# Reordering the start and the row products of a hybrid decoder trunk on one Trainium2 core

## The chip, the cores and the metric

One core of one Trainium2 chip. The metric is device time of one execution in microseconds; lower is better. The kernel before takes 2455.02 us, the median of three runs (2450.69 to 2460.17). Profiles are of one execution of their own.

## What is computed

Two decoder layers on 256 tokens of width 2048, float32, batch 1. Layer 0 mixes tokens with a causal Conformer convolution, layer 1 with gated linear attention; each is followed by a SwiGLU FFN of width 5632. Every sub-layer has a norm before and after it and a modulation (shift, scale, gate) that comes from a vector c:

```python
c_act = silu(c)
for i in range(2):
    mod = c_act @ w_ada[i] + b_ada[i]            # 6 * 2048 values
    sh1, sc1, gt1, sh2, sc2, gt2 = split(mod, 6)
    h = rms_norm(x, pre_mix_g[i]) * (1.0 + sc1) + sh1
    y = conformer_conv(h, ...) if i == 0 else gla_mixer(h, ...)
    x = x + gt1 * rms_norm(y, post_mix_g[i])
    h = rms_norm(x, pre_ffn_g[i]) * (1.0 + sc2) + sh2
    x = x + gt2 * rms_norm(swiglu_ffn(h, ...), post_ffn_g[i])

def conformer_conv(h, ...):
    a, g = split(h @ w_pw1 + b_pw1, 2)           # 2048 -> 2 * 2048
    u = a * sigmoid(g)
    u = depthwise_causal_conv(u, w_dw, width 31) + b_dw
    return silu(layer_norm(u, ln_g, ln_b)) @ w_pw2 + b_pw2
```

Only layer 0's mixer and the modulation vector of layer 0 are touched by the change.

## The kernel before

**Layout.** Activations lie transposed: 128 channels on the partitions, 16 channel blocks (KD), 256 tokens along the free axis. x, y and h are single tiles of this form; h has a high and a low half (`h_hi`, `h_lo`).

**Weights.** All weights come in tiles of 128 x 2048 float32 (1 MB) through one ring of six buffers (`rawp`, tag `raw`). A tile of a product is split into two halves, and each half into a rounded part and a remainder: ScalarE casts `hi` (L318), VectorE subtracts for `lo` (L319). A product is then three matmuls (hi·hi, hi·lo, lo·hi) in a faster float format. `next_half` hands the halves out in order and calls `pump`, which issues tiles a few halves ahead.

**One queue, one order.** All loads are issued from SyncE's queue (SP) in the order that `tile_order` writes out by hand: product tiles (`w`), tiles of w_ada for VectorE (`ada`), tiles of w_ada for TensorE (`rows`), and a few others. `spread` mixes one list evenly into another. Beyond this order a planner with its own cost model arranges the instructions of each engine; `issue_after` and `high_priority` bind it.

**Two ways to a modulation column.** A column is 128 values of mod. On VectorE, an `ada` tile holds 128 columns as rows of 2048, and one SCALAR_TENSOR_TENSOR (L300) multiplies by silu(c), spread over the partitions (`cb`), and sums along the row. On TensorE (`ada_rows`), a unit of two tiles, one pair of columns, is multiplied by silu(c) in 32 copies (`cc`): 16 matmuls of 256 columns into four groups of 32 partitions (L246), a copy to SBUF on ScalarE (L253), two small matmuls with `dup` that add the 32 copies back and turn the result into a column (L255), and an addition of the bias on VectorE (L261). In the head of layer 0 each unit gives block k's shift and scale together, and `modulate` follows (L451, L454, L455).

**Stages of layer 0's mixer.**

1. *Start.* Loads of c, taps, `turn`, x, parameters and bias; the taps are turned into the frequency domain by 12 matmuls on 31 partitions (L571) and stored in y and `h2`; x is squared and summed for the RMS norm (L582 to L592).
2. *Head.* For k = 0..15: row unit k, modulate block k of h, then its part of the three head chunks (4, 0, 5) of pw1. A chunk is 512 output channels; chunks 4 to 7 are the gates.
3. *Tail.* Chunks 1, 6, 2, 7, 3 of pw1, each over all k (L695 to L697). When a pair is done, `transform` makes u = a·sigmoid(g), a forward transform (L616), products with the taps' transform on VectorE (L625 to L633), and an inverse transform (L643 to L645). 18 VectorE columns are spread in between.
4. *LayerNorm* over channels (L707 to L735); row units for gt1 and part of sh2 lie at this place in the order.
5. *pw2* with the remaining row units and VectorE columns spread in; its first eight output blocks run side by side over k, the rest one after another; `gather` collects sums for the norms.
6. *Junction j0*, then FFN 0 and layer 1, which the change leaves as they are.

A row unit from the 17th on is not computed where its tile is issued: it is put on the list `waiting`, and `run_waiting` emits it when the products have come as far.

Of the kernel before, what the change touches and what calls it, by code (L numbers as in the profile page):

```python
# [14 lines left out]
P = 128  # L15
# [73 lines left out]
def tile_order():  # L89
# [6 lines left out]
    def rows(*units):  # L96
        return [("rows", u, half) for u in units for half in range(2)]
# [36 lines left out]
def trunk(ctx: ExitStack, tc: tile.TileContext, a: dict, out: bass.AP):  # L134
# [12 lines left out]
    crow = rawp.tile([P, D], F32, tag="raw", name="crow")  # L147
    nc.sync.dma_start(out=crow[:1, :], in_=a["c"])
# [12 lines left out]
    nc.sync.dma_start(out=x, in_=a["x"])  # L161
# [3 lines left out]
    braw = rawp.tile([P, TILE * P], F32, tag="raw", name="braw")  # L165
    nc.sync.dma_start(out=braw, in_=a["bpw1"])
    masks = const.tile([P, 8, P], I8, tag="masks", name="masks")
    cb = const.tile([P, D], F32, tag="cb", name="cb")
    for j in range(4):
        s = slice(j * 512, (j + 1) * 512)  # L170
        pc = ps.tile([P, 512], F32, tag="mm", name=f"cb{j}")
        nc.tensor.matmul(pc, ones[:1, :], crow[:1, s], start=True, stop=True)
        nc.scalar.activation(out=cb[:, s], in_=pc, func=AF.Silu)
# [25 lines left out]
    y = const.tile([P, KD, T], F32, tag="y", name="y")  # L199
# [38 lines left out]
    def ada_rows(raw, u, half):  # L238
        if half == 0:
            rows[u] = ps2.tile([P, 512], F32, tag="rb" if u < KD and u % 2 else "ss", name=f"ada{u}")  # L240
        bank = rows[u]
        wv = raw.rearrange("p (k n) -> p k n", n=T)
        for i in range(HALF):
            k = half * HALF + i
            j = 32 * (k % 4)
            nc.tensor.matmul(  # L246
                bank[j : j + 32, :T], cc[:, k, :], wv[:, i, :], start=k < 4, stop=k >= KD - 4
            )
        if half == 0:
            return  # L250
        rows.pop(u)
        flat = tmp.tile([P, T], F32, tag="sq", name=f"flat{u}", bufs=3)
        nc.scalar.copy(flat, bank[:, :T])  # L253
        for s in range(2):
            nc.tensor.matmul(  # L255
                bank[:, T + s : T + s + 1], flat[:, s * P : (s + 1) * P], dup, start=True, stop=True
            )
        n0, n1 = ROW_UNITS[u]
        sel = slice(n0, n1 + 1, n1 - n0)
        b_at = COLS["b_ada"][0]  # L260
        nc.vector.tensor_tensor(  # L261
            out=mod[:, sel], in0=bank[:, T : T + 2], in1=par[:, b_at + n0 : b_at + n1 + 1 : n1 - n0], op=ALU.add
        )
        if u < KD:
            nc.vector.scalar_tensor_tensor(
                out=der[:, 0, u : u + 1], in0=modcol(0, n1), scalar=1.0, in1=col("pre_mix_g", u),
                op0=ALU.add, op1=ALU.mult,
            )
            modulate(u, rbx, 0, 0, SH1)
            return  # L270
        have(0, n0 // KD, 2)
# [5 lines left out]
    def pump_one():  # L277
        kind, name, i = order[state["next"]]
        state["next"] += 1
        if kind == "waves":  # L280
            nc.sync.dma_start(out=fwd, in_=a["fwd"])
            nc.sync.dma_start(out=inv, in_=a["inv"])
            return
        raw = rawp.tile([P, TILE * P], F32, tag="raw", name=f"raw{state['next']}")
        if kind == "masks":
# [3 lines left out]
            return  # L289
        if kind == "rows":  # L290
            nc.sync.dma_start(out=raw, in_=a["w_ada_r"][name, i])
            if name < KD:
                ada_rows(raw, name, i)
            else:
                waiting.append((state["emitted"], lambda: ada_rows(raw, name, i)))
            return
        if kind == "ada":
            nc.sync.dma_start(out=raw, in_=a["w_ada"][name, i])
            with tc.issue_after(last_lo[0]) if last_lo else ExitStack():
                nc.vector.scalar_tensor_tensor(  # L300
                    out=raw, in0=raw, scalar=1.0, in1=cb, op0=ALU.mult, op1=ALU.mult, accum_out=modcol(name, i)
                )
            if i % KD == KD - 1:
                first = i - KD + 1
                if (name, i // KD) == (0, SH2):
                    first += sum(n // KD == SH2 for u in ROW_UNITS for n in u)
# [247 lines left out]
    bias_w = cv.tile([P, P], F32R, tag="bias_w", name="bias_w")  # L554
    nc.scalar.activation(out=bias_w, in_=ones, func=AF.Copy, scale=1.0 / 32)
    bias = cv.tile([P, TILE * P], F32R, tag="bias", name="bias")
    fwd = cv.tile([P, 2, F_COLS], F32, tag="fwd", name="fwd")
    inv = cv.tile([P, 3, T], F32, tag="inv", name="inv")
    mean_w = cv.tile([P, 32], F32, tag="mean_w", name="mean_w")
# [6 lines left out]
    for c in range(4):  # L566
        chans = taps[:, c * WIDE : (c + 1) * WIDE]
        for part in range(3):
            n = min(F_MAIN, F_COLS - part * F_MAIN)
# [479 lines left out]
```

## Time and profile before

| | us |
|---|---|
| median of three runs | 2455.02 |
| the profiled execution | 2462.36 |
| its span, first to last instruction | 2460.6 |
| PE busy | 2384.7 (97%) |
| VectorE busy | 1713.8 (70%) |
| ScalarE busy | 1115.1 (45%) |
| mean DMA rate | 246 GB/s |

The span is what the views of the trace count from; the profiled execution's own time is 1.8 us longer. PE's busy time counts pipelined matmuls whose ends are modelled, so a full PE may still have room. In rows of instructions the columns are line, engine, operation, written and read tiles, shapes, count, then busy time, mean nanoseconds of one, and the idle time before it with what ended it. In a timeline they are start, duration, engine, line, operation and tiles, with the idle time and its releaser in brackets. One float32 matmul appears as two records.

### The profile page before, as it was taken

The numbers are of one execution on the slowest core, as the hardware profiler recorded it, in microseconds if no ns is written. First come the engines' busy times: TensorE is split into PE (matmuls) and PEld (weight loads), VectorE is DVE, ScalarE is ACT, GpSimd is POOL, SyncE is SP. The second block draws the span as 40 slices with busy tenths as digits, with TensorE's granted clock in tenths as the row PEclk, the third lists the DMA queues.
The fourth block names the chain that finished last, engine by engine and source line by source line (L and its number), as shares of the span: only waits on it lengthen the run. The fifth ranks groups of instructions, "written<-read, shape, count | busy, mean of one in ns | idle before, by whom it ended". The sixth has DMA issues, their size and how long they took to land.

```text
span 2460.6 us, 35900 instructions
## 1 busy us (share of the span) xinstructions
PE 2384.7 (97%) x14480; PEld 2048.4 (83%) x14480; DVE 1713.8 (70%) x2436; ACT 1115.1 (45%) x1655; POOL 22.0 (1%) x26
## 2 busy tenths in 40 slices
PE   7989989899999999999999999999999999999997
PEld 2667758798888888888888989988988888888886
DVE  2448735887777677778986987898656655665665
ACT  3333325654444444444446545454444444444442
POOL 0000000000000000000000000000000000000001
PEclk9999999999999999999999999998999999999998
DMA  7986776847778778887844566773556656665651
GB/s 250 402 341 250 282 278 242 331 144 289 291 290 295 287 291 294 295 299 291 293 172 145 206 255 237 282 290 135 201 207 223 221 206 220 219 218 202 221 189 67
DMA packets 84504, 606.12 MB, mean 246 GB/s; under 512 B 9507, under 2 KB 9794, under 8 KB 11218
## 3 DMA queue, kind: packets, MB, share of 16 engines
q1 hardware_dynamic: 84338, 603.83, 67.3%
q8 instruction: 113, 1.85, 0.3%
q14 instruction: 53, 0.43, 0.0%
HBM read 601.70 MB, written 2.10 MB: 245 GB/s over the span
## 4 chain that ended last, share of the span: by engine, by line
PE 93%; DVE 3%; DMA 2%; ACT 1%; issue 1%; POOL 0%; POOLq 0%; SPq 0%; DVEq 0%; ACTq 0%
PE in L382 24%; PE out L382 13%; PE in L385 12%; PE out L385 7%; PE pw L695 3%; PE pw L696 2%; PE wo L382 2%; PE pw L697 2%; PE ada L246 2%; PE in_pair L355 1%; PE in_pair L356 1%; PE in_pair L357 1%; PE r L379 1%; PE r L380 1%; PE r L385 1%; PE wo L385 1%
## 5 line engine op out<-in xcount | busy, mean ns | idle before, releaser
L319 DVE TENSOR_TENSOR lo<-raw,hi 128x1024 fp32r<-128x1024 f32 x754 | 921.0, 1223 | 564.4 <-ACT hi L318 562.4
L318 ACT CAST hi<-raw 128x1024 fp32r<-128x1024 f32 x754 | 791.1, 1050 | 1073.3 <-issue 297.0
L382 PE MATMUL in<-h,hi 128*128 128x512 f32 x2560 | 900.0, 397 | 0.0
L385 PE MATMUL in<-h,lo 128*128 128x256 f32 x2560 | 716.3, 280 | 0.0
L382 PEld LDWEIGHTS in<-h,hi 128*128 128x128 f32 x2560 | 480.8, 188 | 117.4
L385 PEld LDWEIGHTS in<-h,lo 128*128 128x128 f32 x2560 | 482.8, 189 | 0.0
L382 PE MATMUL out<-m,hi 128*128 128x512 f32 x1364 | 477.3, 394 | 0.0
L385 PE MATMUL out<-m,lo 128*128 128x256 f32 x1408 | 392.0, 281 | 0.0
L300 DVE SCALAR_TENSOR_TENSOR raw<-raw,cb 128x2048 f32<-128x2048 f32 x136 | 310.6, 2284 | 4.8 <-DMA raw<-in_w_ada_dram 4.8
L382 PEld LDWEIGHTS out<-m,hi 128*128 128x128 f32 x1364 | 254.9, 188 | 58.4
L385 PEld LDWEIGHTS out<-m,lo 128*128 128x128 f32 x1408 | 264.1, 188 | 2.0
L695 PE MATMUL pw<-hi,h 128*128 128x512 f32 x256 | 101.9, 411 | 9.7 <-ACT h L454 9.7
L696 PE MATMUL pw<-lo,h 128*128 128x512 f32 x256 | 103.7, 406 | 0.0
L697 PE MATMUL pw<-hi,h 128*128 128x512 f32 x256 | 90.4, 396 | 0.0
L382 PE MATMUL wo<-oo,hi 128*128 128x512 f32 x240 | 83.7, 394 | 0.0
L355 PE MATMUL in_pair<-h,hi 128*128 128x256 f32 x256 | 71.4, 293 | 2.9 <-ACT h L454 2.9
L385 PE MATMUL r<-h,lo 128*128 128x256 f32 x256 | 73.2, 286 | 0.0
L379 PE MATMUL r<-h,hi 128*128 128x256 f32 x256 | 73.1, 286 | 0.0
L380 PE MATMUL r<-h,hi 128*128 128x256 f32 x256 | 72.9, 285 | 0.0
L356 PE MATMUL in_pair<-h,hi 128*128 128x256 f32 x256 | 72.6, 290 | 0.0
L695 PEld LDWEIGHTS pw<-hi,h 128*128 128x128 f32 x256 | 49.3, 193 | 27.2 <-ACT h L454 13.9
L385 PE MATMUL wo<-oo,lo 128*128 128x256 f32 x256 | 71.2, 281 | 0.0
(349 smaller groups left out, 2997.9 us busy)
## 6 DMA issues: line engine op xcount, KB each, us to landing
raw<-in_in_dram SPq DMA_DIRECT2D x176, 1024.0 KB, 5.0
raw<-in_w_ada_dram SPq DMA_DIRECT2D x136, 1024.0 KB, 5.3
raw<-in_out_dram SPq DMA_DIRECT2D x88, 1024.0 KB, 5.0
raw<-in_w_ada_r_dram SPq DMA_DIRECT2D x56, 1024.0 KB, 7.2
raw<-in_pw_dram SPq DMA_DIRECT2D x48, 1024.0 KB, 6.7
raw<-in_aqk_dram SPq DMA_DIRECT2D x17, 1024.0 KB, 4.9
raw<-in_v_dram SPq DMA_DIRECT2D x16, 1024.0 KB, 6.1
raw<-in_r_dram SPq DMA_DIRECT2D x16, 1024.0 KB, 5.8
```

The lines of the kernel that those rows point to most:

```text
L300: nc.vector.scalar_tensor_tensor(out=raw, in0=raw, scalar=1.0, in1=cb, op0=ALU.mult, op1=ALU.mult, accum_out=modcol(name, i))
L318: nc.scalar.copy(hi, part)
L319: done = nc.vector.tensor_tensor(out=lo, in0=part, in1=hi.bitcast(F32), op=ALU.subtract)
L355: nc.tensor.matmul(acc, w_hi, x_hi, start=opens, stop=False, skip_group_check=True)
L356: nc.tensor.matmul(acc, w_hi, x_lo, start=False, stop=False, skip_group_check=True)
L379: nc.tensor.matmul(acc[:, :T], w_hi[:, s], x_hi, start=n == 0, stop=False)
L380: nc.tensor.matmul(acc[:, :T], w_hi[:, s], x_lo, start=False, stop=False)
L382: nc.tensor.matmul(acc, w_hi[:, s], pair.rearrange("p a b -> p (a b)"), start=n == 0, stop=end, skip_group_check=True)
L385: nc.tensor.matmul(acc[:, :T], w_lo[:, s], x_hi, start=False, stop=end, skip_group_check=ob not in narrow)
L695: nc.tensor.matmul(accs[c][t], h_hi[:, k, n], w_hi[:, s], start=False, stop=False)
L696: nc.tensor.matmul(accs[c][t], h_hi[:, k, n], w_lo[:, s], start=False, stop=False)
L697: nc.tensor.matmul(accs[c][t], h_lo[:, k, n], w_hi[:, s], start=False, stop=k == KD - 1)
```

## The change

- **Loads first.** c goes into a part of y instead of a ring buffer; x follows at once, in four transfers. taps, `turn` and the bias of pw1 are issued between the k-tiles of the head, and the sums of squares of x use y as scratch, so that none of them takes a ring buffer at the start. taps and `turn` get a 32nd row of zeros. The bias comes as four rows into a tile that GpSimd has filled with zeros, and is added by a matmul in the middle of each accumulation (k = 12) instead of at its beginning.
- **Taps in the head.** The 12 taps matmuls become four steps (`taps_chunk`) after k = 4, 6, 8 and 10.
- **Scale on VectorE, shift on TensorE.** A row unit is now one tile with one column: 16 matmuls of 128 columns, one `dup` matmul. The 16 sh1 columns and the 16 gt1 columns go this way (32 units). The 16 sc1 columns, sc2 and sh2 go over VectorE: 16 in the head, 22 in pw1's tail, 10 in pw2.
- **Row products behind the inverse transform.** Six gt1 units are spread into the tail, four stand at its end and are held until the last inverse transform's last matmul, six lie in pw2. The last transform's inverse uses another PSUM bank.
- u, the gates' sigmoids and the taps share one tile (`share`).

```diff
-ROW_UNITS = [(k, KD + k) for k in range(KD)]
-ROW_UNITS += [(GT1 * KD + k, GT1 * KD + k + 1) for k in range(0, KD, 2)]
-ROW_UNITS += [(SH2 * KD + k, SH2 * KD + k + 1) for k in range(0, 8, 2)]
+ROW_COLS = [SH1 * KD + k for k in range(KD)] + [GT1 * KD + k for k in range(KD)]
...
     order = []
+    extra = {0: ["taps"], 2: ["waves"], 4: ["turn"], 5: ["bias"], 6: ["turn"], 8: ["turn"], 10: ["turn"]}
     for k in range(KD):
-        order += rows(k)
+        order += [("ada", 0, SC1 * KD + k)] + rows(k)
         order += [pw1[i] for i in range(lead) if 4 * i // len(HEAD_CHUNKS) == k]
-        if k == 2:
-            order += [("waves", 0, 0)]
-    late = ada(0, SC2) + ada(0, SH2)[8:]
-    units = range(KD, len(ROW_UNITS))
-    order += spread(pw1[lead:], late[:18])
-    order += rows(*units[:6])
-    order += spread(pw2[:12], rows(*units[6:]) + late[18:], 4) + pw2[12:]
+        order += [(kind, k, 0) for kind in extra.get(k, ())]
+    late = ada(0, SC2) + ada(0, SH2)
+    units = rows(*range(KD, len(ROW_COLS)))
+    order += spread(pw1[lead:], spread(late[:22], units[:6]), 1)
+    order += units[6:10] + spread(pw2[:14], units[10:] + late[22:], 2) + pw2[14:]
...
+    y = const.tile([P, KD, T], F32, tag="y", name="y")
+    crow = y[:1, KD // 2 :, :].rearrange("p a b -> p (a b)")
+    nc.sync.dma_start(out=crow, in_=a["c"])
...
-    taps = rawp.tile([P, TILE * P], F32, tag="raw", name="taps")[:WIDTH, :]
-    nc.sync.dma_start(out=taps, in_=a["taps"])
-    turn = early.tile([P, F_COLS], F32, tag="turn", name="turn")[:WIDTH, :]
-    nc.sync.dma_start(out=turn, in_=a["turn"])
...
-    nc.sync.dma_start(out=x, in_=a["x"])
+    for j in range(4):
+        nc.sync.dma_start(out=x[:, 4 * j : 4 * j + 4, :], in_=a["x"][:, 4 * j : 4 * j + 4, :])
...
-    braw = rawp.tile([P, TILE * P], F32, tag="raw", name="braw")
-    nc.sync.dma_start(out=braw, in_=a["bpw1"])
...
+    def ada_rows(raw, u):
+        bank = ps2.tile([P, 512], F32, tag="rb" if u < KD and u % 2 else "ss", name=f"ada{u}")
+        wv = raw.rearrange("p (k n) -> p k n", n=P)
+        for k in range(KD):
             j = 32 * (k % 4)
+            nc.tensor.matmul(bank[j : j + 32, :P], cc[:, k, :], wv[:, k, :], start=k < 4, stop=k >= KD - 4)
+        flat = tmp.tile([P, T], F32, tag="sq", name=f"flat{u}", bufs=3)[:, :P]
+        nc.scalar.copy(flat, bank[:, :P])
+        nc.tensor.matmul(bank[:, P : P + 1], flat, dup, start=True, stop=True)
+        n = ROW_COLS[u]
+        nc.vector.tensor_tensor(out=modcol(0, n), in0=bank[:, P : P + 1], in1=col("b_ada", n), op=ALU.add)
...
+        if kind == "taps":
+            nc.sync.dma_start(out=taps, in_=a["taps"])
+            nc.sync.dma_start(out=turn, in_=a["turn"])
+            return
+        if kind == "turn":
+            taps_chunk(turned.pop(0))
+            return
...
+        if kind == "bias":
+            nc.gpsimd.memset(raw, 0.0)
+            nc.sync.dma_start(out=raw[::32, :], in_=a["bpw1"])
+            nc.scalar.copy(bias, raw)
+            nc.vector.tensor_tensor(
+                out=bias[64:, :], in0=raw[64:, :], in1=bias[64:, :].bitcast(F32), op=ALU.subtract
+            )
+            return
...
+            if (name, i // KD) == (0, SC1):
+                k = i % KD
+                nc.vector.scalar_tensor_tensor(
+                    out=der[:, 0, k : k + 1], in0=modcol(0, i), scalar=b1[:, k : k + 1], in1=col("pre_mix_g", k),
+                    op0=ALU.add, op1=ALU.mult,
+                )
+                return
...
-            back = ps2.tile([P, 512], F32, tag="ss", name=f"back{half}")
+            if c == TAIL_CHUNKS[-1]:
+                back = ps.tile([P, 512], F32, tag="mm", name=f"back{half}")
+            else:
+                back = ps2.tile([P, 512], F32, tag="ss", name=f"back{half}")
...
-            u = cv.tile([P, 2, T], F32, tag="u", name=f"u{half}", bufs=2)
+            u = share[:, 2 * j * T : 2 * (j + 1) * T].rearrange("p (t n) -> p t n", t=2)
...
-    run_waiting(state["used"])
     while order[state["next"]][0] == "rows":
         pump_one()
-        if len(waiting) > 2:
-            waiting.pop(0)[1]()
-    run_waiting(state["used"])
+    with tc.issue_after(ends["inverse"]):
+        run_waiting(state["used"])
```

`taps_chunk` holds the three taps matmuls of one chunk of 512 channels and their copies on ScalarE, on the two PSUM banks that the row units use.

More of the change, by code (lines that the diff above doesn't have):

```diff
@@ L96, in rows @@
     def rows(*units):
-        return [("rows", u, half) for u in units for half in range(2)]
+        return [("rows", u, 0) for u in units]
     pw1, pw2 = w("pw1"), w("pw2")
@@ L171, in trunk @@
         pc = ps.tile([P, 512], F32, tag="mm", name=f"cb{j}")
-        nc.tensor.matmul(pc, ones[:1, :], crow[:1, s], start=True, stop=True)
+        nc.tensor.matmul(pc, ones[:1, :], crow[:, s], start=True, stop=True)
         nc.scalar.activation(out=cb[:, s], in_=pc, func=AF.Silu)
@@ L264, in ada_rows, with taps_chunk @@
         if u < KD:
[L265 to L268, printed above, removed]
             modulate(u, rbx, 0, 0, SH1)
-            return
-        have(0, n0 // KD, 2)
+        else:
+            have(0, n // KD, 1)
+    def taps_chunk(c):
+        chans = taps[:, c * WIDE : (c + 1) * WIDE]
+        for part in range(3):
+            n = min(F_MAIN, F_COLS - part * F_MAIN)
+            pt = ps2.tile([P, WIDE], F32, tag="rb" if part % 2 else "ss", name=f"taps{c}{part}")[:n, :]
+            nc.tensor.matmul(pt, turn[:, part * F_MAIN : part * F_MAIN + n], chans, start=True, stop=True)
+            if part == 2:
+                nc.scalar.copy(h2[:, c * WIDE : (c + 1) * WIDE], pt)
+            else:
+                nc.scalar.copy(
+                    y[:, 4 * c : 4 * c + 4, part * P : (part + 1) * P], pt.rearrange("p (b n) -> p b n", n=P)
+                )
@@ L552, in junction @@
         gate[:] = [end.ins]
-    bias_w = cv.tile([P, P], F32R, tag="bias_w", name="bias_w")
-    nc.scalar.activation(out=bias_w, in_=ones, func=AF.Copy, scale=1.0 / 32)
+    both_w = cv.tile([P, 2, P], F32, tag="both_w", name="both_w")
+    nc.vector.memset(both_w, 0.0)
+    for q in range(4):
+        nc.vector.memset(both_w[32 * q : 32 * q + 1, q % 2, :], 1.0)
+    bias_w = cv.tile([P, 2, P], F32R, tag="bias_w", name="bias_w")
+    nc.scalar.copy(bias_w, both_w)
     bias = cv.tile([P, TILE * P], F32R, tag="bias", name="bias")
@@ L558, in trunk @@
     inv = cv.tile([P, 3, T], F32, tag="inv", name="inv")
+    turn = cv.tile([P, F_COLS], F32, tag="turn", name="turn")[:32, :]
+    share = cv.tile([P, D], F32, tag="share", name="share")
+    taps = share[:32, :]
+    turned = list(range(4))
     mean_w = cv.tile([P, 32], F32, tag="mean_w", name="mean_w")
@@ L564, in trunk @@
         nc.vector.memset(v2[4 * F_REST : 4 * F_REST + 32, :], -1.0 / 32)
[L566 to L569, printed above, removed]
-            pt = ps.tile([P, WIDE], F32, tag="mm", name=f"taps{c}{part}")[:n, :]
-            nc.tensor.matmul(pt, turn[:, part * F_MAIN : part * F_MAIN + n], chans, start=True, stop=True)
-            if part == 2:
-                nc.scalar.copy(h2[:, c * WIDE : (c + 1) * WIDE], pt)
-            else:
-                nc.scalar.copy(
-                    y[:, 4 * c : 4 * c + 4, part * P : (part + 1) * P], pt.rearrange("p (b n) -> p b n", n=P)
-                )
-    sqs = [rawp.tile([P, TILE * P], F32, tag="raw", name=f"sqs{j}") for j in range(2)]
-    quarter = [sqs[j // 2][:, (j % 2) * 4 * T : (j % 2 + 1) * 4 * T] for j in range(4)]
+    quarter = [y[:, 4 * j : 4 * j + 4, :] for j in range(4)]
     for j in range(4):
-        nc.scalar.square(quarter[j], x[:, 4 * j : 4 * j + 4, :].rearrange("p a b -> p (a b)"))
+        nc.scalar.square(quarter[j], x[:, 4 * j : 4 * j + 4, :])
         if j % 2:
@@ L644, in inverse @@
                     nc.tensor.matmul(yi, vb[:, i, :], inv[:, 1, :], start=False, stop=False)
-                    nc.tensor.matmul(yi, v2[:rows, sel], inv[:rows, 2, :], start=False, stop=True)
+                    return nc.tensor.matmul(yi, v2[:rows, sel], inv[:rows, 2, :], start=False, stop=True)
                 if b == 0:
@@ L685, in trunk @@
                 accs[c] = [ps.tile([P, 512], F32, tag="mm", name=f"pw1_{c}{t}") for t in range(2)]
-            q = 64 * (c // 4)
-            for t in range(2):
-                nc.tensor.matmul(
-                    accs[c][t], bias_w[q : q + 64, :], bias[q : q + 64, c % 4 * WIDE : (c % 4 + 1) * WIDE],
-                    start=True, stop=False,
-                )
         s = slice(idx % 2 * WIDE, (idx % 2 + 1) * WIDE)
```

72 lines of the change are left out of this document (22 added, 50 removed).

## The prediction

> **What bounds the kernel now.** First the busy time by stage, cut where the work changes: first product of the conformer's pw1, end of its head chunks, last pw1 product, first and middle of pw2, the junction to the FFN. Columns: stretch, length, busy time and instructions of PE, PE weight loads, VectorE (DVE), ScalarE (ACT) and, in most, GpSimd, granted clock, DMA share, GB/s.
>
> ```profile
> 0.00:59.00 59.00, 44.22 (x149) 15.26 (x149) 15.61 (x25) 24.06 (x34) 0.91 (x5) 1.00 0.69 246
> 59.00:173.70 114.70, 104.04 (x761) 74.39 (x761) 47.02 (x86) 36.27 (x53) 0.00 (x0) 0.97 0.96 376
> 173.70:328.70 155.00, 155.00 (x683) 118.11 (x684) 111.87 (x155) 55.75 (x73) 0.00 (x0) 1.00 0.74 267
> 328.70:372.10 43.40, 31.84 (x281) 19.15 (x280) 18.67 (x49) 11.46 (x21) 0.69 (x1) 0.97 0.77 290
> 372.10:428.00 55.90, 55.90 (x484) 51.15 (x481) 29.17 (x43) 28.81 (x49) 0.00 (x0) 0.96 0.65 238
> 428.00:487.00 59.00, 53.02 (x345) 44.04 (x344) 51.61 (x91) 35.92 (x67) 0.00 (x0) 0.94 0.89 346
> 499.00:2460.60 1961.60, 1932.30 (x11742) 1719.58 (x11742) 1431.84 (x1970) 917.96 (x1353) 18.84 (x18) 0.99 0.65 234
> ```
>
> From 499 us on nothing is edited, and PE is full: 1961.6 us that stay. What counts is how early 499 is reached. The first 59 us hold no product; the head (59 to 173.7) is bound by DMA (96%) with PE close behind; the tail by PE; the 43.4 us around the LayerNorm by waits; the second half of pw2 has VectorE at 51.6 of 59.
>
> Why the start takes 59 us: DMA by short stretches, then x's transfer (microseconds to landing last) and the timeline of what hangs on it.
>
> ```profile
> 5.00:9.00 4.00, 4.00 (x6) 1.31 (x4) 0.00 (x0) 2.24 (x4) 0.00 (x0) 1.00 0.99 401
> 16.00:18.00 2.00, 0.00 (x0) 0.00 (x0) 0.00 (x0) 0.00 (x0) 0.00 (x0) 1.00 0.10 36
> 28.00:30.00 2.00, 0.44 (x2) 0.43 (x2) 1.33 (x2) 2.00 (x5) 0.00 (x0) 1.00 0.06 25
> x<-in_x_dram SPq DMA_DIRECT2D x1, 2048.0 KB, 22.9
> 20.37 6.79 PE L571 MATMUL taps<-taps,turn 31*128 31x512 f32 x7 [10.64 <-DMA turn<-in_turn_dram]
> 25.16 1.06 ACT L582 ACTIVATE sqs<-x 128x1024 f32<-128x1024 f32 x1 [14.79 <-DMA x<-in_x_dram]
> L584 DVE TENSOR_TENSOR sqs<-sqs 128x1024 f32<-128x1024 f32 x2 | 2.5, 1225 | 26.1 <-ACT sqs L582 26.1
> 36.94 0.42 DVE L588 TENSOR_TENSOR s_xx<-sqs 128x256 f32<-128x256 f32 x1
> 42.22 1.01 PE L407 MATMUL ssx<-inv_d,s_xx 128*128 128x1 f32 x4
> 43.51 0.70 POOL L417 TENSOR_TENSOR nx_r<-nx_r,mhalf 128x2 f32<-128x2 f32 x1 [43.07 <-DVE nx_r L438]
> 50.91 1.22 PE L433 MATMUL nx_rb<-nx_dg,ones 128*128 128x256 f32 x2
> 58.96 0.48 PE L695 MATMUL pw<-hi,h 128*128 128x512 f32 x1
> ```
>
> DMA ran at 401 GB/s at 5 to 9 us, yet the 2 MB of x counted as landed only 25.1 us in. At 16 to 18 and 28 to 30 us the share is 0.10 and 0.06, at 36 and 25 GB/s: one engine of sixteen (1/16 = 0.0625) still draining while fifteen are done. Ahead of x stand the taps and turn, on 31 partitions; I read them as having gone to that one engine, so x's last packets queue behind them. By the Trainium skill ("DMA: Bandwidth & Descriptors", section "Why a DMA increments its semaphore by 16 and not by 1") a transfer uses the largest number of engines, at most 16, that divides its outermost sizes: one for 31 rows, sixteen for the new 32. By that rule x lands at full rate after the change.
>
> Then, between s_xx and the first product, PE is in order: 24 taps records of 1.1 us stand around the statistics' short matmuls.
>
> **The change, part by part.**
>
> *Start.* x is issued third, in four quarters; taps, turn and bias move behind k-tiles; the six raw slots are free at once. x: issue at 1.5, 2.1 MB at 401 GB/s = 5.2, and an allowance of mine of 1.9 to begin and end: landed by 8.6. Then, by the rows above: squares of the last quarters to 11 (ACT also makes silu(c)), adds 1.23, 1.23, 0.69, 0.42 to 14.6, sums 1.0, the power with its neighbours 0.9, the diagonal 0.4, its product 1.2, a copy 0.4, two modulate steps 1.0: about 19.5. One VectorE scale op ahead of it (2.3) makes the first product 22, where it was 59. Bounds: 19 and 36 (x still at 25).
>
> *Head.* Rows of prices, grouped over 59 to 173.7 us, but the taps (0 to 59) and L300 (the page's groups); then DMA over 60 to 140:
>
> ```profile
> L246 PE MATMUL ada<-raw,cc 128*32 128x256 f32 x416 | 26.4, 383 | 0.0
> L255 PE MATMUL ada<-dup,flat 128*128 128x1 f32 x57 | 7.5, 233 | 1.0 <-ACT flat L253 1.0
> L451 DVE SCALAR_TENSOR_TENSOR mt<-x,der,s_xz 128x256 f32<-128x256 f32 x15 | 7.2, 483 | 0.5
> L319 DVE TENSOR_TENSOR lo<-raw,hi 128x1024 fp32r<-128x1024 f32 x22 | 26.8, 1223 | 30.0 <-ACT hi L318 30.0
> L300 DVE SCALAR_TENSOR_TENSOR raw<-raw,cb 128x2048 f32<-128x2048 f32 x136 | 310.6, 2284 | 4.8 <-DMA raw<-in_w_ada_dram 4.8
> L571 PE MATMUL taps<-taps,turn 31*128 31x512 f32 x16 | 15.8, 1114 | 12.2 <-DMA turn<-in_turn_dram 10.6 <-ACT y L575 1.6
> 59.44 0.23 PE pw L696
> 60.00:140.00 80.00, 75.59 (x593) 54.34 (x591) 32.95 (x61) 25.91 (x38) 0.00 (x0) 1.00 1.00 404
> ```
>
> The head still loads 32 ada and 12 pw1 tiles of 1.05 MB, plus 1.0 MB of taps, turn, waves and bias: 47.2 MB at 404 GB/s = 117 us. From 9.4 us (x, par, ident in) that is 126; with 8 to 12 us to work off the last tiles, 134 to 138. The bias tile waits for a slot and a GpSimd fill on SP's queue, with every later load behind it; what it adds is covered by the tiles in flight, or costs a tile's 2.6 us at most.
>
> PE: 288 products at the 0.23 step = 66. A row unit was 32 records of 256 columns plus four of L255 and three switches of about 0.35, near 2.9; half as many columns, two L255 records and two switches make 2.0. The half-width form is in no row; its bounds come from one unit cut finely (counts are records under way):
>
> ```profile
> 341.62:341.66 0.04, 0.03 (x4) 0.03 (x4) 1.00 0.99 410
> 341.66:341.87 0.21, 0.21 (x4) 0.13 (x8) 1.00 0.96 390
> 341.87:341.90 0.03, 0.03 (x8) 0.02 (x4) 1.00 0.64 273
> ```
>
> Four start together, nothing more for 0.21 us, then the next four: eight groups of 0.216 = 1.73, paced by the stream of 256 columns, and the weight loads inside take 0.13. So halving goes down to about 0.13 a group (1.1 a unit) at best and stays at 1.9 at worst; I take 1.1, since no issue rate shows inside a group. Sixteen units: 32. Taps: 24 records; on a full-speed PE perhaps 0.45 each, as they were 1.1; with copies 12, at most 26. Bias 1.4. PE's sum is 111, from 22 us on: 133. VectorE: 16 scale ops of 2.36 with the accumulator read (38), modulations 20, lo 29, statistics 5, bias 2: 94 of some 115. All three near 134; head's end 138, bounds 130 and 152, where it was 173.7: **-36**.
>
> *Tail.* Where the row units' records (32 a unit) lie now, for L246 alone: stretch, length, PE and weight loads, clock, DMA.
>
> ```profile
> 173.70:328.70 155.00, 2.58 (x36) 1.09 (x38) 1.00 0.74 267
> 372.10:428.00 55.90, 7.38 (x100) 2.93 (x96) 0.96 0.65 238
> 428.00:487.00 59.00, 3.87 (x64) 1.87 (x64) 0.94 0.89 346
> ```
>
> 22 instead of 18 VectorE columns: +9.4, into 43 us of VectorE idle. Six row units instead of about one, on a PE without idle: 6 x 2.0 less 3, and banks shared with the back transforms, 1 to 2: **+8** (0 to +15).
>
> *LayerNorm.*
>
> ```profile
> 338.15 0.41 DVE L631 TENSOR_TENSOR vb<-vb,vy 128x256 f32<-128x256 f32 x1
> 338.28 1.93 PE L246 MATMUL ada<-raw,cc 128*32 128x256 f32 x32 [0.40 <-DVE mod L261]
> 348.45 0.70 PE L643 MATMUL back<-inv,va 128*128 128x256 f32 x2 [0.32 <-DVE mod L261]
> 367.42 0.42 DVE L446 TENSOR_TENSOR h<-lt,h 128x256 fp32r<-128x256 f32 x1
> 370.31 1.94 PE L246 MATMUL ada<-raw,cc 128*32 128x256 f32 x16 [3.61 <-DMA raw<-in_w_ada_r_dram]
> 372.17 1.23 PE L355 MATMUL pw_pair<-h,hi 128*128 128x256 f32 x4
> ```
>
> The last inverse transform has its inputs at about 338.5 and starts at 348.45, three row units and their loads ahead of it in PE's order. Held behind the last inverse, rows no longer do that: -10. Another row's load held pw2 from 367.8 to 372.2; now four preloaded units sit in the LayerNorm's shadow, about 2.5 each in series for one bank, 10 in a shadow of 10: between -4 and +3, I take -1. **-11** (-14 to -6).
>
> *pw2.* First half: six units at 2.0 for three at 2.9: +3. Second half: two units fewer (-6), but ten VectorE columns instead of six (+9.4) where 7.4 us of VectorE are idle: +5 taken (-4 to +12). **+2**.
>
> Sum: -36 +8 -11 +2 = **-37**. Profiled execution: 2462.4 (span 2460.6 + 1.8), so 2425; it stood 7.3 above the median 2455.0, so on the runs' scale **2418**.
>
> **Rivals.**
>
> *VectorE paces everything (slower).* It is in order and takes 24 columns more: 24 x 2.36 = 56.6. If each stands ahead of something PE needs (its der, its lo), the sum is -37 + 56.6 = +20: 2475. It decides where added work passes idle time: head 38 against 67, tail 9.4 against 43, only pw2's second half has too little. Planner's order speaks for it, these margins against. Chance 0.07.
>
> *VectorE paces pw2 only*: a lag of 20 there instead of 5, with GT1 late for the gathers: 2433. 0.12.
>
> *Half-width rows cost as much as full ones.* A unit stays 1.9: +0.8 on 32 units, of which head, tail and pw2 carry 28: +22, and the LayerNorm shadow overflows by 3: 2443. The finely cut rows speak against it. 0.10. A rule of the skill would give it: "TensorE: Matmul & The Clock Gate", section "Wait — 56ns, not 53.3ns?", has an issue cost of about 62 ns per matmul when the hardware decoder is off, so 32 records would take about 2.0 us at any width; four starting within 0.04 us disagree.
>
> *x lands no earlier* (the late engine had another cause): first product at 36, tiles stall on full slots meanwhile, head's end 150: 2430. The 0.06 share behind x speaks against. 0.06.
>
> **How the numbers follow.** Forecast 0.65, its own range 2398 to 2436 (head 130 to 150, the others half their bounds). With the milder rivals the range is 2396 to 2446; below it and above it lie under 2 in 10. Half a per cent, 12 us, is about what a measurement can tell: the line is at 2443. Faster: 0.62 of the forecast, most of pw2 and x, half of the rows: 0.85. Same 0.08, slower 0.07.
>
> **What would show it.** x's landing near 7 us from issue; first pw1 product near 22, last head product near 138; DMA near 400 GB/s from 5 us on; L246 units near 1.1; no row record between the last fab and the last back product; VectorE under 90% outside pw2's second half. Wrong if the head lasts over 130 us from its first product (rows or VectorE), or if 499 moves less than the head's end does by over 15 (tail or pw2).

## The result, and the profile after

The changed kernel takes 2418.69 us, the median of four runs from 2408.62 to 2420.36; the kernel before took 2457.47 in the same session (four runs, 2450.69 to 2460.17). The ratio is 0.9838, with a 95% interval from 0.9803 to 0.9873: 1.6% faster. The forecast was 2418, in a range from 2396 to 2446. The execution profiled is the fastest of the four, 2408.62 us with a span of 2406.8, so its rows hold some 10 us less than the median.

The table of stages of the changed kernel, cut at the same places as that of before: first pw1 product, end of the head chunks, last pw1 product, first packed product of pw2, middle of pw2, first product of the FFN. The columns are those of the first table in the prediction.

```profile
0.00:23.20 23.20, 11.48 (x48) 6.10 (x48) 12.76 (x30) 13.75 (x18) 0.91 (x5) 1.00 0.90 324
23.20:146.50 123.30, 109.56 (x828) 77.19 (x829) 83.41 (x118) 43.97 (x69) 1.81 (x1) 0.97 0.99 391
146.50:302.00 155.50, 155.50 (x811) 122.22 (x810) 120.31 (x165) 56.92 (x77) 0.00 (x0) 1.00 0.84 313
302.00:331.70 29.70, 27.01 (x274) 20.82 (x272) 15.73 (x45) 9.72 (x20) 0.69 (x1) 0.83 0.69 245
331.70:384.50 52.80, 52.79 (x522) 50.93 (x522) 36.01 (x54) 29.19 (x51) 0.00 (x0) 1.00 0.74 258
384.50:453.30 68.80, 56.92 (x340) 48.30 (x338) 64.00 (x118) 40.53 (x74) 1.54 (x2) 0.90 0.80 292
453.30:2406.80 1953.50, 1924.64 (x11742) 1717.27 (x11742) 1432.03 (x1970) 917.46 (x1352) 18.84 (x18) 0.99 0.65 235
```

The first product comes at 23.2 us where it came at 59.0. From there the head takes longer than before, 123.3 us for 114.7, though its DMA share is 0.99. The tail is as long as it was, the stretch around the LayerNorm shrinks from 43.4 to 29.7, and pw2 with the junction behind it is some 5 us shorter. The FFN's first product, at 499 before, comes at 453.3.

What lies behind it, in the changed kernel: x's four transfers (median microseconds to landing last), and from PE's timeline (start, duration, instruction) the statistics, the first product, and a row unit in the tail with what stands next to it.

```profile
x<-in_x_dram SPq DMA_DIRECT2D x4, 512.0 KB, 4.8
17.29 1.01 PE L413 MATMUL ssx<-inv_d,s_xx 128*128 128x1 f32 x4 [7.56 <-DVE s_xx L587]
23.21 0.80 PE L688 MATMUL pw<-hi,h 128*128 128x512 f32 x1 [1.30 <-ACT h L460]
299.41 0.39 PE L694 MATMUL pw<-hi,h 128*128 128x512 f32 x1
299.73 1.08 PE L235 MATMUL ada<-raw,cc 128*32 128x128 f32 x32
300.74 0.50 PE L688 MATMUL pw<-hi,h 128*128 128x512 f32 x1
302.23 0.28 PE L238 MATMUL ada<-dup,flat 128*128 128x1 f32 x2
302.37 0.68 PE L612 MATMUL fab<-share,fwd 128*128 128x256 f32 x2
```

Three of x's quarters land 5.6, 6.9 and 8.4 us into the span; the fourth has no landing record, but ScalarE squares it from 10.4 us on without a wait. A row unit takes PE 1.0 us and its two dup records 0.14, 1.15 in all. At a switch between products and a row unit the step is 0.32 to 0.34 us (299.41 to 299.73, 300.74 to 301.08), where the products step by 0.23.

### The profile page after: what moved, and what is told of

The parts are those of the page before. It is cut to its first block, busy times and chain, and to the rows that moved or that the text cites. A ratio compares the mean times of both kernels' runs of the same rounds, so it can differ in the third digit from the quotient of the medians.

```text
span 2406.8 us, 36099 instructions
## 1 busy us (share of the span) xinstructions
PE 2337.9 (97%) x14560; PEld 2042.8 (85%) x14560; DVE 1764.2 (73%) x2493; ACT 1111.5 (46%) x1659; POOL 23.8 (1%) x27
## 4 chain that ended last, share of the span: by engine, by line
PE 79%; DVE 1%; ACT 0%; POOL 0%; issue 0%; POOLq 0%
PE in L388 25%; PE out L388 13%; PE in L391 12%; PE out L391 7%; PE wo L388 2%; PE in_pair L361 1%; PE in_pair L362 1%; PE in_pair L363 1%; PE r L385 1%; PE r L386 1%; PE r L391 1%; PE wo L391 1%; PE v L887 1%; PE v L888 1%; PE v L886 1%; PE s L837 1%
## 5 line engine op out<-in xcount | busy, mean ns | idle before, releaser
L301 DVE SCALAR_TENSOR_TENSOR raw<-raw,cb 128x2048 f32<-128x2048 f32 x160 | 365.3, 2284 | 4.4 <-DMA raw<-in_w_ada_dram 4.0
```

What stands on the lines that cost most here:

```text
L301: nc.vector.scalar_tensor_tensor(out=raw, in0=raw, scalar=1.0, in1=cb, op0=ALU.mult, op1=ALU.mult, accum_out=modcol(name, i))
```

## The experiments

One table carries most of what follows. Each trace is cut at the same records: first pw1 product, first product of the tail chunks, last pw1 product, first and last packed product of pw2, first packed product of the FFN. All are lengths in us but for the two ends; "rest" is the same work in every kernel. "ratio" is to the kernel before in the same session, with its 95% interval.

```
                  start  head (end)     tail   LN    pw2a  pw2b+junction  rest    ratio
before             59.0  115.5 (174.5)  153.6  44.1  57.6  69.4           1961.4
changed            23.2  123.7 (146.9)  154.9  29.9  52.6  69.0           1953.5  0.9838 [0.9803, 0.9873]
after_again        23.8  124.9 (148.7)  154.9  33.0  53.4  69.0           1953.4  0.9823 [0.9799, 0.9847]
pad_only           46.2  118.6 (164.9)  153.6  46.1  55.7  69.3           1955.5  0.9939 [0.9922, 0.9957]
rows_31            23.3  140.3 (163.6)  154.9  30.0  52.8  67.7           1961.8  0.9878 [0.9854, 0.9903]
no_hold            23.6  126.9 (150.5)  154.9  30.1  53.4  69.0           1963.5  0.9827 [0.9799, 0.9854]
back_ss_no_hold    23.3  125.1 (148.4)  154.9  41.9  53.5  69.2           1951.1  0.9870 [0.9846, 0.9893]
narrow_scale       24.3  125.2 (149.5)  154.9  32.7  52.6  70.4           1955.5  0.9830 [0.9806, 0.9854]
slots5             24.0  121.7 (145.6)  157.8  33.0  52.8  72.2           1957.1  0.9829 [0.9805, 0.9853]
rows4              24.0  119.4 (143.4)  154.8  28.5  53.4  70.4           1958.1  0.9821 [0.9794, 0.9848]
half_loads         26.6  111.3 (138.0)  154.6  28.5  53.3  70.5           1955.2  0.9792 [0.9768, 0.9815]
rows_spread        23.5  124.8 (148.2)  154.9  32.9  53.4  69.0           1957.2  0.9830 [0.9807, 0.9853]
spread2            23.4  125.1 (148.5)  154.9  28.3  55.5  70.4           1957.7  0.9851 [0.9822, 0.9881]
both_moves         23.3  124.7 (148.0)  158.9  27.0  56.5  60.2           1960.5  0.9802 [0.9774, 0.9830]
```

**The same kernel again (after_again).**

> The changed kernel once more, nothing edited, for a second profile beside the kernel before. In the first pair of profiles the stretch from the first FFN product to the end, which the change does not touch, was 1953.5 us after and 1961.6 us before; 3.8 us of that lay in each of the two first halves of an FFN's in-product (199.3 for 203.1 us). If that is a difference between executions, this profile shows the stretch anywhere from 1953 to 1962 us and the time within 2408 to 2421. The rival, that the edits reach into the FFN by way of the order of work, has 199.3 us in both first halves again and the whole stretch at 1953 to 1955 us.

The rest is 1953.4 us again, as the rival had it. But no_hold (below), whose instructions turned out to stand in the order of the changed kernel, has 1963.5. The two halves in question, FFN 0's and FFN 1's first in-products, first in the changed kernel, then in no_hold:

```profile
502.20:701.50 199.30, 199.30 (x1152) 174.29 (x1151) 157.56 (x190) 97.41 (x147) 0.00 (x0) 1.00 0.80 293
1694.60:1894.00 199.40, 199.40 (x1153) 175.83 (x1152) 125.68 (x158) 97.44 (x147) 0.00 (x0) 1.00 0.62 217
```

```profile
506.60:709.80 203.20, 203.20 (x1153) 176.21 (x1152) 157.59 (x190) 97.45 (x147) 0.00 (x0) 1.00 0.79 288
1704.80:1907.90 203.10, 203.10 (x1152) 176.22 (x1151) 125.58 (x158) 97.44 (x147) 0.00 (x0) 1.00 0.61 213
```

One order of work, a full PE and a granted clock of 1.00 in both, yet two paces 2% apart. So this part differs between executions, and the 8 us that the first pair of profiles shows there need not be the change's (pad_only, below, has 1955.5 in the order of before). Stages are therefore compared one by one, not by the ends of spans.

**One row more in before (pad_only).** The kernel before with this alone:

```
-    taps = rawp.tile([P, TILE * P], F32, tag="raw", name="taps")[:WIDTH, :]
+    taps = rawp.tile([P, TILE * P], F32, tag="raw", name="taps")[: WIDTH + 1, :]
-    turn = early.tile([P, F_COLS], F32, tag="turn", name="turn")[:WIDTH, :]
+    turn = early.tile([P, F_COLS], F32, tag="turn", name="turn")[: WIDTH + 1, :]
```

(with a row of zeros and one more lag in the arrays).

> The kernel before with one edit: taps and turn are padded from 31 to 32 rows with a row of zeros (and an unused lag), order of loads as it was. If the 31 rows went to one engine and x's last packets queued behind them, x's transfer lands by 8 to 10 us instead of 25.1, the first pw1 product starts at 41 to 46 us instead of 59, the end of the head moves by as much, and the time falls by 11 to 17 us. Rival, that x was late for its place in the queue or another cause: x at 22 to 26 us, first product 57 to 60, time within 4 us of before.

From the list of transfers, PE's timeline and the DMA by stretches of this kernel:

```profile
x<-in_x_dram SPq DMA_DIRECT2D x1, 2048.0 KB, 8.9
46.24 0.48 PE L695 MATMUL pw<-hi,h 128*128 128x512 f32 x1
16.00:18.00 2.00, 2.00 (x4) 0.66 (x2) 1.93 (x3) 2.00 (x3) 0.00 (x0) 1.00 1.03 430
```

x lands 8.9 us after its issue instead of 22.9, and the DMA share at 16 to 18 us is 1.03 where it was 0.10. The first product comes 12.7 us earlier, just past the edge of what was expected, and the time falls by 0.61%, 15 us of 2458. Expected was that the end of the head moves by as much as its beginning: by the profiles 9.6 of the 12.7 us are left there, and as many at the FFN's first product. So a 32nd row of zeros is worth about a third of what the whole change brings by the medians, and a fifth to a quarter by the stages.

**31 rows in the changed kernel (rows_31).** The changed kernel with the opposite edit:

```
-    turn = cv.tile([P, F_COLS], F32, tag="turn", name="turn")[:32, :]
+    turn = cv.tile([P, F_COLS], F32, tag="turn", name="turn")[:WIDTH, :]
-    taps = share[:32, :]
+    taps = share[:WIDTH, :]
```

(with the arrays back on 31 rows).

> The changed kernel with taps and turn back on 31 rows, issued where the change put them (behind the first k-tile). By the one-engine reading that engine gets 0.29 MB that the sixteen would have shared, at 25 GB/s some 11 us more than its share: the tiles loaded at 7 to 20 us count as landed about 11 us late, the head's end moves from 146.5 to 152 to 158 us, and the time rises by 5 to 11 us. x, which stands ahead of them, still lands by 9 us and the first product stays near 23. Rival: the rows are spread over the engines all the same, nothing moves by over 2 us.

Waits of PE and of VectorE in the head of this kernel (total us, times, longest):

```profile
PE ada L235 <- DMA raw<-in_w_ada_r_dram: 12.4, 2, 11.3
...
DVE raw L301 <- DMA raw<-in_w_ada_dram: 14.2, 2, 13.8
```

One row unit and one scale column of an early k each stand over 11 us for tiles loaded behind the taps, and the head is 15 to 17 us longer. That is more than either wait; PE's granted clock was also lower, 0.50 over 30 to 40 us and 0.74 over 80 to 100. The ratio rises from 0.9823 to 0.9878, 13.5 us, more than expected: the whole delay reaches the end of the head, and nothing behind it makes it good. x, ahead of the taps in the queue, is not touched, and the first product stays at 23.3.

**Rows not held (no_hold), and the bank besides (back_ss_no_hold).** The first edit alone, then both:

```
-    with tc.issue_after(ends["inverse"]):
-        run_waiting(state["used"])
+    run_waiting(state["used"])
```

```
-            if c == TAIL_CHUNKS[-1]:
-                back = ps.tile([P, 512], F32, tag="mm", name=f"back{half}")
-            else:
-                back = ps2.tile([P, 512], F32, tag="ss", name=f"back{half}")
+            back = ps2.tile([P, 512], F32, tag="ss", name=f"back{half}")
```

> The changed kernel with the row units before pw2 not held behind the last inverse transform: they stand where the planner puts them. The prediction gave the hold 10 us: the stretch from the last pw1 product to the first pw2 product goes from 29.7 to 38 to 41 us, row records stand between the last forward and the last inverse transform again, and the time rises by 8 to 11 us. Rival: the held units stand in the LayerNorm's own chain (its sums and their squares behind row units and their copies, some 5 us), so that the hold is worth only the difference: the stretch goes to 32 to 36 us, the time up by 2 to 6.

> The changed kernel with two edits of its last inverse transforms undone: their banks are again those that the row units use, and the rows are not held. Undoing the hold alone left the stretch from the last pw1 product to the first pw2 product at 30.1 us. If the bank carried the gain, row units stand ahead of the inverse transforms again: the stretch goes to 36 to 41 us and the time rises by 6 to 11. Rival: the gain came from there being fewer and narrower row units there: 29 to 33 us, the time within 3.

Without the hold nothing changes: the stretch is 30.1 us, the ratio 0.9827, and the instructions of this part stand in the same order; the planner puts the rows behind the inverse transforms by itself. Neither theory had that. With the bank undone as well the stretch is 41.9 us and the time 11.5 us longer (0.9870 for 0.9823); it differs from no_hold by the bank alone. PE's timeline of that kernel:

```profile
312.03 1.08 PE L235 MATMUL ada<-raw,cc 128*32 128x128 f32 x32 [0.60 <-DVE mod L240]
...
314.36 1.88 PE L235 MATMUL ada<-raw,cc 128*32 128x128 f32 x32 [0.48 <-DVE mod L240]
...
317.66 1.22 PE L639 MATMUL back<-inv,va 128*128 128x256 f32 x2 [0.42 <-DVE mod L240]
...
321.15 1.22 PE L639 MATMUL back<-inv,va 128*128 128x256 f32 x2 [0.56 <-ACT y L652]
...
328.14 1.22 PE L639 MATMUL back<-inv,va 128*128 128x256 f32 x2 [0.56 <-ACT y L652]
```

Steps of the same four transforms in the changed kernel, then in the kernel before:

```profile
312.49 0.59 PE L642 MATMUL back<-inv,va 128*128 128x256 f32 x2
313.79 0.60 PE L642 MATMUL back<-inv,va 128*128 128x256 f32 x2
```

```profile
351.67 0.70 PE L643 MATMUL back<-inv,va 128*128 128x256 f32 x2 [1.65 <-ACT y L656]
354.39 0.70 PE L643 MATMUL back<-inv,va 128*128 128x256 f32 x2 [1.16 <-ACT y L656]
```

With the bank undone, two row units more stand ahead of the last inverse transforms, which start 14.2 us behind the last pw1 product instead of 7.6. Then each transform waits for ScalarE to have emptied the one bank, and a step takes 3.5 us where the changed kernel takes 1.3 to 1.5. The wait is only 0.56 us of that: the records themselves last nearly twice as long (1.22 for 0.70 us), at a granted clock of 0.50 over 317.6 to 331 us, where the changed kernel has 1.00 over its inverse transforms. At the full clock, in the kernel before, steps on the one bank take 2.1 to 3.2 us. That the hold alone would do, with the bank undone, was not tried.

**Where the head's time goes (narrow_scale, slots5, rows4, half_loads).** Four edits of the changed kernel. The scale columns of the head reduced over 32 of 2048 weights; five raw slots; a quarter of the head's row records; half of each scale column's load. All but slots5 leave out a part of layer 0's modulation, so they can only measure.

```
+                n = 32 if (name, i // KD) == (0, SC1) else D
-                    out=raw, in0=raw, scalar=1.0, in1=cb, op0=ALU.mult, op1=ALU.mult, accum_out=modcol(name, i)
+                    out=raw[:, :n], in0=raw[:, :n], scalar=1.0, in1=cb[:, :n], op0=ALU.mult, op1=ALU.mult,
+                    accum_out=modcol(name, i),
```

```
-    rawp = ctx.enter_context(tc.tile_pool(name="rawp", bufs=6))
+    rawp = ctx.enter_context(tc.tile_pool(name="rawp", bufs=5))
```

```
         for k in range(KD):
             j = 32 * (k % 4)
+            if u < KD and k >= 4:
+                continue
...
```

```
+            n = D // 2 if (name, i // KD) == (0, SC1) else D
-            nc.sync.dma_start(out=raw, in_=a["w_ada"][name, i])
+            nc.sync.dma_start(out=raw[:, :n], in_=a["w_ada"][name, i][:, :n])
...
```

> The changed kernel with the sixteen scale columns of the head reduced on VectorE over 32 of their 2048 weights (all loads stay; the other 2016 terms of layer 0's sc1 are left out): 16 x 2.26 = 36 us of VectorE work gone from the head. Theory: VectorE, in order, gives raw slots back late and stands ahead of the additions that free the row banks, and this is what made the head last 123 us instead of 115 and the DMA rate fall to 370 GB/s after 80 us. Then the rate is 395 or more again over 80 to 130 us, the head lasts 111 to 115 us and the time falls by 7 to 12 us. Rival: PE's own 110 us of work in order with the loads is the limit: the head stays at 120 us or more, the time within 4.

> The changed kernel with five raw slots instead of six. If in the head the loads wait for slots that come back late (a loop of 6 x 1.05 MB per 17 us at 370 GB/s), five give 5/6 of it, 308 GB/s over 80 to 140 us: the head's end moves from 147 to 165 to 172 us and the time rises by 18 to 25. Rival: the transfers themselves are the limit and slots are only taken earlier than needed: the head's end moves by less than 5 us.

> The changed kernel with the sixteen row units of the head on 8 records each instead of 32 (k below 4 of 16; every load stays; three quarters of layer 0's sh1 are left out): 16 x 0.8 = 13 us of PE work gone from the head, nothing else. With the wide scale work gone and with five slots the head's length had not changed. Theory: PE, in order, is the limit (110 us busy and 14 us waiting in 123): the head lasts 108 to 114 us and the time falls by 9 to 14. Rival: the loads are the limit (48 MB at 400 GB/s from 5 us on, to 125, and the drain): the head lasts 117 us or more and the time falls by at most 6.

> The changed kernel with each of the sixteen scale columns of the head loaded and reduced over 1024 of its 2048 weights (the other half of layer 0's sc1 is left out): 16 x 0.52 = 8.4 MB of 46 MB of tiles gone, 21 us at 400 GB/s, and half the scale work, which had made no difference when nearly all of it was gone. PE's work is as it was. In every kernel so far the last tiles of the head came in at 125 to 131 us, and the head ended 13 to 16 us later. Theory: the loads set when the last k-tiles can start, and PE comes next: the last tiles land at 108 to 115 us, the head ends at 135 to 140 instead of 145 to 147 (PE's 110 us from 23 on, with its waits), the time falls by 6 to 11 us. Rival: the chain of each k on PE, in order (row unit, ScalarE's copy, VectorE's addition, modulation, products; 7.3 to 7.7 us a step), is the limit whatever the loads do: the head ends at 143 or later, the time within 4.

The head's row in the table of stages, first of narrow_scale:

```profile
24.30:149.50 125.20, 111.81 (x830) 78.51 (x831) 52.82 (x116) 44.40 (x69) 1.80 (x1) 0.95 0.98 385
```

of rows4:

```profile
24.00:143.40 119.40, 104.08 (x470) 70.64 (x471) 81.52 (x117) 44.48 (x69) 1.81 (x1) 0.93 0.99 398
```

and of half_loads, with all of its waits of PE in that stretch:

```profile
26.60:138.00 111.40, 107.11 (x802) 76.35 (x799) 67.06 (x113) 45.12 (x69) 1.81 (x1) 0.97 0.93 359
PE pw L690 <- ACT h L462: 2.5, 2, 1.5
PE ada L235 <- ACT h L253: 0.7, 2, 0.4
PE ada L235 <- DMA raw<-in_w_ada_r_dram: 0.4, 1, 0.4
PE ada L238 <- ACT flat L237: 0.4, 1, 0.4
```

The first two theories fall. VectorE goes from 83 to 53 busy us in the head, and the head stays at 125. With five slots it ends at 145.6, no later than with six, and the ratio is 0.9829; the planner's order moved with the slots, and the tail and the last stage are some 3 us longer each (157.8 and 72.2). Taking 12 us of row records off PE (360 at 34 ns) shortens it by 4 to 6, so that its rival (a head of 117 us or more) stood; but PE's busy time fell by only 6, at a granted clock of 0.93 for 0.97, so that this run is no clean test of PE. Halving the scale columns' loads shortens it by 12 to 14, to 111.4, and there PE is nearly full: 107.1 us busy and 4 us of waits, where the changed kernel had 14. The head begins 3 us later, so that its end comes 9 to 11 us earlier, at 138.0. VectorE's work on these columns is halved with the loads, but narrow_scale had taken nearly all of it away without effect. The last two tiles landed at 117.5 and 119.5 us, later than the 108 to 115 expected, where they landed at 127.5 and 130.0 in the changed kernel. So the loads set the end of the head in the changed kernel, and PE is next, some 10 us behind.

**Rows kept out of the LayerNorm (rows_spread, spread2, both_moves).** The first puts the call that runs the held rows behind the spread product in the program's text:

```
-    with tc.issue_after(ends["inverse"]):
-        run_waiting(state["used"])
         both = spread_tokens([rl, mr], "nl")
+        run_waiting(state["used"])
```

PE's order stayed as it was, so the run is one more of the same order. spread2 orders the held units behind that product's instruction, ahead of pw2:

```
+            ends["spread"] = nc.tensor.matmul(rb[:, j * T : (j + 1) * T], ones, spread_one(r, f"{name}{j}"), start=True, stop=True).ins
...
-    with tc.issue_after(ends["inverse"]):
-        run_waiting(state["used"])
...
+    with tc.issue_after(ends["spread"]):
+        run_waiting(state["used"])
```

both_moves does the same, and loads the tail's rows and six more VectorE columns earlier:

```
-    order += spread(pw1[lead:], spread(late[:22], units[:6]), 1)
-    order += units[6:10] + spread(pw2[:14], units[10:] + late[22:], 2) + pw2[14:]
+    order += spread(pw1[lead:], spread(late[:20], units[:6]) + late[20:28], 1)
+    order += units[6:10] + spread(pw2[:6], units[10:], 1) + spread(pw2[6:14], late[28:]) + pw2[14:]
```

> The changed kernel with the row units that were held behind the last inverse transform held longer, behind the product that spreads the LayerNorm's statistics. In the changed kernel two to three units and their copies (ScalarE, in order ahead of the squares l_sq) stand inside the LayerNorm's chain at half clock. If they cost it 4 to 8 us, the stretch from the last pw1 product to the first pw2 product goes from 30 to 33 us to 23 to 27 and the time falls by 4 to 8. Rival: the units then stand ahead of pw2's first products, 4 x 2.5 us in series for one bank: the stretch stays or grows to 36, and the time changes by -2 to +5.

> The changed kernel with the last held row units issued behind the product that spreads the LayerNorm's statistics, by an explicit order after that product's instruction (in the run before it their order had not changed). In the first profile of the changed kernel one unit stood between the sums and the spread product on PE and one ahead of the sums besides those that are older in the order. Theory: they cost the chain 2 to 4 us at half clock: the stretch from the last pw1 product to the first pw2 product falls from 30 to 33 us to 27 to 30, pw2's first half takes one to two units more (53 to 55 us), and the time changes by -3 to 0. Rival: the chain is set by ScalarE's squares and the copies of the two older units ahead of them, which stay: stretch 30 to 33, time within 2, or up by 3 where the units in pw2's first half cost PE more.

> The changed kernel with two moves: (a) as the run above, with the six row units of the tail loaded earlier so that none is left ahead of the LayerNorm's last sums; (b) 28 instead of 22 of the VectorE columns of layer 0 in the tail, so that 4 instead of 10 stand in pw2's second half. Theory: (a) gives 4 to 6 us in the stretch between pw1 and pw2 (30 to 33 us to 25 to 28), (b) frees 14 us of VectorE in pw2's second half, where it was busy 57.6 of 59.4 us: that half falls to 53 to 56 us; the tail, with 14 us more of VectorE work in 35 us of its idle time, grows by 0 to 3: time 5 to 11 us below the changed kernel. Rival: the tail's transforms wait for VectorE and the loads of the six tiles take DMA time from pw1's: tail +5 to +10, the time unchanged or up.

rows_spread has a stretch of 32.9 us and 0.9830, within what the same order gives. spread2 brings the stretch to 28.3 and pays in pw2's first half, 55.5: the two together are 83.8 us, between the 82.5 and 86.4 of the changed kernel's two profiles, and its ratio of 0.9851 is no gain. The four stages of both_moves, from the tail on:

```profile
148.00:306.90 158.90, 157.45 (x844) 122.88 (x843) 131.91 (x176) 55.46 (x78) 0.00 (x0) 1.00 0.90 333
306.90:333.90 27.00, 21.57 (x171) 14.94 (x170) 16.63 (x43) 8.62 (x17) 0.70 (x1) 0.88 0.68 268
333.90:390.40 56.50, 56.50 (x624) 54.18 (x624) 35.45 (x59) 31.03 (x58) 0.00 (x0) 1.00 0.80 286
390.40:450.50 60.10, 52.53 (x306) 46.02 (x305) 52.21 (x103) 38.72 (x70) 1.54 (x2) 0.91 0.61 222
```

Its last stage falls from 69.0 to 60.1 us as VectorE's work there falls from 64.0 to 52.2. The places of loads and row units moved with it, but in the changed kernel no wait of that stage ended on a load, and only one row unit (1.1 us) stood in it. So VectorE paces that stage. The tail gives 4 back, pw2's first half 3 to 4. The ratio, 0.9802, lies 0.2% below the changed kernel's 0.9823 and inside its interval: it points to a gain of some 5 us, which these runs do not tell from none.

## Why the prediction was right, and where it was not

The time came out as forecast because errors of both signs met; that it lies within 1 us is luck. The head's end was forecast 8 to 10 us too early; the tail and pw2 some 7 us each too long, the LayerNorm up to 3. By the records of the table above: up to the FFN's first product the forecast was -37; the two profiles of the changed kernel have -45.9 and -40.1, and the medians of the two sessions 38.8 and 44.1 less. Two sums of the prediction don't come out as it has them: the tail's terms (12 less 3, and 1 to 2) make 10 to 11 and not 8, and half the bounds put its own range at about 2400 to 2440, not 2398 to 2436.

*Start: right.* 23.2 for 22, with three quarters of x landed by 8.4 (8.6 was allowed for all). That the 31 rows are the cause is shown: pad_only takes the delay out with one row, and rows_31 puts one in. That they go to one engine is read from the share of one sixteenth; no view names the engine. This is also the rule that the Trainium skill has in "DMA: Bandwidth & Descriptors", section "Why a DMA increments its semaphore by 16 and not by 1"; the traces agree (22.9 against 8.9 us for x), and the rival "x lands no earlier" falls.

*Head: mechanism half right, size wrong.* The end fell by 27.6 and 25.8, not by 36. The failed step is "with 8 to 12 us to work off the last tiles, 134 to 138", and the last tile at 126. Measured, the last column and weight tiles landed at 130.0 and 127.5 us (the last row tile, issued at 125.5, has no record of it), at a DMA rate of 391 and not 404 GB/s over the head, and the head ended 16.5 us after that. PE's first products of the last k-steps start at 128.2, 135.5 and 142.5 us: a step takes 7 us in order (eighteen products, the next row unit, the wait for its shift and modulation), and two of them follow the last landing. PE's sum of 111 was right to 2% (109.6 busy), but by luck of two terms: from each record's start to the next, without idle time, the products took 74.4 for 66 and the fifteen row units of the stretch 20.5 for sixteen at 32 (taps 13.4 for 12). And the prediction took the latest of three engines that each end near 134, where loads and PE's steps follow each other. VectorE, the third of them, had no part (narrow_scale).

*Half-width rows: right, and better.* 1.08 us for a unit's 32 records, 34 ns each, for 1.1 taken; with its dup records 1.15, where 2.0 was counted. That rival falls, and with it the 2.0 us that the prediction made of the figure in the Trainium skill, "TensorE: Matmul & The Clock Gate", section "Wait — 56ns, not 53.3ns?", by counting 62 ns for each record. Counted by the program's sixteen matmuls, two records each, the trace has 68 ns, which does not contradict that figure; it is for the hardware decoder off, and no run here shows whether that is so.

*Tail: too dear.* +1.3 for +8. The step that failed is "6 x 2.0 less 3": a unit in a full PE costs 1.15, a switch some 0.1 (0.32 to 0.34 for 0.23) and not 0.35, and by the row of L235 alone in the tail (records of PE, then weight loads) five of the six stood there:

```profile
146.90:301.80 154.90, 5.41 (x160) 4.06 (x160) 1.00 0.84 313
```

The 9 us of added VectorE work were covered, as said.

*LayerNorm: size right, cause wrong.* -14.2 and -11.1 for -11. Row units ahead of the last inverse transforms do cost what was said, but "Held behind the last inverse, rows no longer do that" is not what takes them away: no_hold has the same order. It is the edit that gives the last inverse transforms banks of their own, which the prediction did not price: with it undone too, 12 us come back. One row unit (307.55 us) and its dup records (310.97) do stand between the last forward and the last inverse transforms, against the sign given.

*pw2: wrong sign.* -5.4 and -4.6 with the junction, for +2. In the first half PE has no idle time in any of the three profiles, so that its records tell all of it. "Six units at 2.0 for three at 2.9" failed as in the tail: row units took 5.1 us there (four of the six, and one's dup records) for 8.3 before. And a second thing was not seen: the products took 47.6 (48.3 in after_again) for 49.3, because before, PE came out of the LayerNorm's waits to half the clock. From before, from the changed kernel and from after_again, the granted clock (third from the right) of the stretch where it fell:

```profile
366.00:378.00 12.00, 8.39 (x65) 6.59 (x53) 6.82 (x15) 5.99 (x13) 0.00 (x0) 0.72 0.60 214
```

```profile
319.00:330.00 11.00, 9.95 (x94) 8.19 (x86) 3.18 (x13) 3.42 (x8) 0.69 (x1) 0.53 0.78 271
```

```profile
334.00:338.00 4.00, 3.64 (x41) 3.07 (x40) 3.77 (x10) 2.65 (x7) 0.00 (x0) 0.50 0.72 252
```

Before, it reached 4.5 us into pw2's first products; in the changed kernel's first profile it lies in the LayerNorm's shadow, and pw2 begins at full speed. In after_again, the same kernel, it lasts 2.2 us into pw2. So its place differs between executions, and it is worth 1 to 2 of the 4 to 5 us by which the first half is shorter. In the second half the four VectorE columns more and the two units fewer cancel; no run tells them apart. There the rival "VectorE paces pw2 only" had its mechanism right (both_moves), but VectorE was busy 51.6 of 59 us there already before, and the stage came out no longer.

The rival "VectorE paces everything" fell with narrow_scale and with VectorE's 77% in the tail. In the head, SyncE's queue waits for slots that PE and VectorE give back (up to 7.3 and 6.5 us at a time in the changed kernel), but neither five slots nor nearly no scale work on VectorE moved the head's end by more than 4 us; what holds the DMA rate at 391 GB/s stays open.

## What to carry to other kernels

Look for a transfer that lands late while the DMA share sits at one sixteenth, and for row counts such as 31, where one row of zeros makes 32. Where several engines each add up to nearly the same end, add the last steps that follow the last load; don't take the latest of the sums. Before crediting an order edit, look whether the planner already had that order, and whether a shared bank is what really forced it.

## What the runs showed that was not expected

The same PE-full stretch of some 1152 records takes 199.3 or 203.1 us at a granted clock of 1.00, by execution, and the two FFNs of one execution need not agree (in pad_only 199.3 and 203.2). One raw slot of six could be taken away at no cost that the time shows (slots5, 0.9829). And where the half-clock stretch falls matters: in the LayerNorm's waits it lengthens 1.08 us units to 1.94, in pw2 it costs products, and two executions of the same kernel had 10.2 and 17.1 us of it around the LayerNorm.
